# Thirteen places of twelve matmuls for the local branch's output products, and a shorter sum in the final norm

## The chip, the cores and the metric

The kernel runs on one core of a Trainium2 chip. A core has a matrix engine (TensorE, in the profile PE, its weight loads PEld), an engine for elementwise work and reductions (VectorE, DVE), one for activation functions and copies (ScalarE, ACT), a general one (GpSimd, POOL), and one that issues transfers (SyncE, SP). They run side by side and wait for one another by semaphores. Matmuls write to PSUM, which is handed out here in banks of 128 x 512 float32; everything else lives in SBUF.

The metric is the device time of the whole program in microseconds, the median of several runs. Before the change it is 1325.01 us (three runs: 1324.27, 1325.01 and 1326.56).

## The reference

One decoder layer on a sequence of 1024 positions with 1024 channels, all in float32, with two attention branches that are mixed by gates. Cut to what matters:

```
h = rmsnorm(x, mix_norm_g)
qa, ka, va, q_lat, kv_lat, k_r, g_a, g_b = split(h @ w_in)
o_a = sliding-window attention of qa, ka, va          # "local", 8 heads of 64
o_b = causal latent attention, 8 heads, softmax over all earlier positions
y   = sigmoid(g_a) * (o_a @ w_o_swa) + sigmoid(g_b) * (o_b @ w_o_mla)
x   = x + y @ w_out
h   = rmsnorm(x, ffn_norm_g)
x   = x + (silu(h @ w_gate) * (h @ w_up)) @ w_down
out = x * rsqrt(mean(x * x) + 1e-6) * final_norm_g
```

The change touches the product `o_a @ w_o_swa` with its gate `sigmoid(g_a)`, in its place in the program alone, and the last line.

## The kernel before

**Products in three passes.** Every float32 operand is split into a high part and a rest (`split`: ScalarE copies, line 163, VectorE subtracts, line 166), and `mm3` (lines 172 to 174) makes three matmuls of each pair: high by high, high by rest, rest by high. A product of 128 x 512 over 512 input channels is therefore twelve matmuls of 512 columns.

**The latent steps.** After the projections and the local attention the kernel goes through the latent attention in 64 steps `t`: 8 heads `h` by 8 query blocks of 128, where `n = t % 8` counts the steps of a head. The blocks of a head are taken in the order 2, 3, 6, 7, 0, 1, 4, 5, so a step handles between 128 and 1024 key positions. In program order a step does this:

- `scores(t + 2)`: the scores of the step after next on TensorE (lines 1253 to 1255) into one of two double banks of PSUM (`scb`); VectorE adds the mask and takes the row maximum in one instruction (line 1263), ScalarE takes the exponential and its sum (1264), GpSimd the reciprocal of the sum as a power (1265) and scales the probabilities `p` with it (1266).
- `pv` for a pair of blocks whose `p` was transposed some steps earlier (lines 1302, 1303, the result in `ob`).
- in certain steps, part of a unit of the local branch's output product (`mix_a`, matmuls into `oA`).
- `transposes(t)`: the blocks of `p` of this step by TensorE (line 1280, into `pTb`), then the split by ScalarE and VectorE (`pth`, `ptl`).
- loads and conversions for later steps.

So the softmax of a step runs on VectorE, ScalarE and GpSimd while TensorE does the work of two steps, and the transposition is where TensorE comes back to its result.

**The local branch's output products.** There are 16 units `(dc, sh)`: 8 blocks of 128 output channels by 2 halves of the positions, twelve matmuls each. When a unit is complete, VectorE multiplies it by the gate in one instruction (line 1359; the gate tile `sg` holds tanh(g / 2), to which 1 is added, twice the sigmoid). Thirteen units lie among the latent steps, three behind them or in the last step. In the kernel before each of the thirteen is cut in two halves of six matmuls (`c0 = 0` and `c0 = 2`), and the 26 halves have places in the dictionary `fill`: steps 5 and 6 of head 0; n = 1, 2, 5 and 6 of heads 1, 3 and 5; n = 1, 2 and 5 of heads 2, 4, 6 and 7. Between its halves a unit keeps its bank, one of the four of the pool `P1`, which also serves `pTb` and `ob`.

For every other unit a new gate tile is loaded (`load_sig`, line 1333, 512 KB, dictionary `g_at`, at the place ahead of the unit's first) and ScalarE turns it into the tanh (`twice_sigmoid`, line 1336) in the unit's first step, behind the transpositions. The weights come in four pieces, loaded six steps and converted two steps ahead of the unit that first uses them (`w_at`).

**Order.** In this stretch the order of the instructions on each engine isn't written out by hand. A planner makes it at compile time from the program order and its own estimate of the durations, and an instruction that it takes to be ready can be put ahead of an earlier one. Instructions traced under `held[0] = True` keep their program order. On the chip each engine then runs its list strictly in that order.

**The end.** The last stage is the product with `w_down`, in seven products of half size (`ORDER` is 1, 6, 2, 7, 5, 4, 3). When the products 4 and 3 are through, each of four tiles of 128 rows goes through the final norm (`down_done`, `final`): VectorE adds the residual (line 180), ScalarE squares one half of the channels and sums (1931), GpSimd divides by 1024 and adds the other half's sum, which already holds the epsilon (1936), GpSimd takes the power -1/2 (1937), then VectorE and ScalarE multiply one half each (1939, 1942), and both are stored. The other half's sum was prepared by `first_half` at products 2 and 5.

Of the kernel before, what the change touches and what calls it, by code (L numbers as in the profile page):

```python
# [8 lines left out]
F32 = mybir.dt.float32  # L9
# [8 lines left out]
P = 128  # L18
S = 1024
D = 1024  # L20
# [69 lines left out]
def hybrid_block_kernel(  # L90
# [53 lines left out]
    def U(name, dt=F32, shape=(P, 1024)):  # L144
        return pool.tile(list(shape), dt, tag="u", name=uid(name))
# [7 lines left out]
    def P1(name, shape=(P, 512), dt=F32):  # L153
        return ps1.tile(list(shape), dt, tag="ps", name=uid(name))
# [212 lines left out]
    def bcast_gain(name, g, w=1024):  # L367
        t = U(name)
        nc.sync.dma_start(t[:, 0:w], g.partition_broadcast(P))
        return t  # L370
# [964 lines left out]
    def twice_sigmoid(g):  # L1335
        a = nc.scalar.activation(g, g, AF.Tanh, scale=0.5)
        if held[0]:
            tc.keep_in_program_order(a)
# [4 lines left out]
    def mix_a(dc, sh, c0, n, ps=None):  # L1343
        if ps is not None:
            oa_ps[(dc, sh)] = ps
        ps = oa_ps[(dc, sh)]
        if (sh, c0) == (0, 0):
            if dc >= 4:
                ar[dc] = gate[dc]
            elif dc % 2 == 0:  # L1350
                t = V("ar", F32, (P, 2, S))
                ar[dc], ar[dc + 1] = t[:, 0], t[:, 1]
            if dc % 2 == 0:
                wo[dc // 2] = st.get(("oa", dc // 2))
        w = wo[dc // 2]
        mm3(ps, [((w[0][:, c, blk(dc % 2)], w[1][:, c, blk(dc % 2)]), oaT[(c, sh)]) for c in range(c0, c0 + n)],
            c0 == 0, c0 + n == 4)
        if c0 + n == 4:
            nc.vector.scalar_tensor_tensor(ar[dc][:, half(sh)], gate[dc][:, half(sh)], 1.0, oa_ps.pop((dc, sh)),
                                           op0=ALU.add, op1=ALU.mult)  # L1360
            if sh == 1:
                gate.pop(dc)
                if dc >= 4:
                    nc.sync.dma_start(ar_d[dc - 4], ar.pop(dc))
# [55 lines left out]
    load_k(2)  # L1420
    first = {0: (2, 0), 1: (2, 1), 2: (3, 0), 3: (3, 1)}
    fill = {}
    units = [(u // 2 ^ 4, u % 2, c) for u in range(16 - 3) for c in (0, 2)]
    slots = [5, 6] + [NB * h + n for h in range(1, NH) for n in (1, 2, 5, 6) if n < 6 or h in (1, 3, 5)]
    for t, u in zip(slots, units):
        fill[t] = u
    w_at = {t: u[0] // 2 for t, u in fill.items() if u[0] % 2 == 0 and u[1:] == (0, 0)}
    g_at = {a: fill[b][0] for a, b in zip([3] + slots, slots) if fill[b][1:] == (0, 0)}
    g_at[NT - 3] = 3
    pvq = []  # L1430
    OUT_AT = {34: 0, 40: 1, 43: 2, 47: 3, 50: 4, 54: 5, 58: 6}
    for t in range(NT):
        h, n = divmod(t, NB)
        if t + 2 < NT:
            scores(t + 2)
        while pvq and pvq[0][0] <= t:
            pv(*pvq.pop(0)[1:])
        if n == 4 and h + 2 < NH:
            load_q(h + 2)
        if n == 6 and h + 3 < NH:  # L1440
            load_k(h + 3)
        hh, nn = step(t)
        if nn % 2 == 1:
            pvq.append((t + 3, hh, nn // 2))
        e = t - (NT - 8)
        if e == 6:
            psum_phase("psc", 4)
        if t in first:
            prod_k(*first[t])
        if t in fill:  # L1450
            dc, sh, c0 = fill[t]
            mix_a(dc, sh, c0, 2, P1("oA") if c0 == 0 else None)
        if t == NT - 1:
            mix_a(13 // 2 ^ 4, 13 % 2, 0, 4, PX("oA"))
        transposes(t)
        if t in OUT_AT:
            out_sums(OUT_AT[t])
        held[0] = True
        if t in g_at:
            load_sig(g_at[t])  # L1460
        if t in fill and fill[t][1:] == (0, 0):
            twice_sigmoid(gate[fill[t][0]])
        if t == NT - 1:
            twice_sigmoid(gate[3])
        if t == 3:
            load_oa(0, 1)
            load_oa(1, 1)
        if t < 4 or 6 <= t < 10:
            split_oa(t % 4 // 2 if t < 4 else (t - 6) // 2, t // 6, t % 2)
        if t + 6 in w_at or t == 0:  # L1470
            st.load_to(st.index[("oa", w_at.get(t + 6, 2))])
        if t + 2 in w_at:
            st.conv_to(st.index[("oa", w_at[t + 2])])
        if e == 4:
            load_sigs(DCS[0])
        if -3 <= e < 3:
            split_ob((e + 3) // 2, (e + 3) % 2)
        if e in (2, 6):
            st.load_to(st.index[("ob", 0 if e == 2 else 2)])
        if e == 6:  # L1480
            st.conv_to(st.index[("ob", 0)])
        held[0] = False
# [441 lines left out]

    p1, u2, u3 = V("dp1"), V("du2"), V("du3")
    fing = bcast_gain("fing", fin_g)
    fin_s = const.tile([P, 2, 2, 4], F32, name="fin_s")

    def sumsq(i, d, t):
        junk = U("sq", F32, (P, 512))  # L1930
        nc.scalar.activation(junk, xq[(i, d)][:, t], AF.Square, accum_out=fin_s[:, i, d, t:t + 1])

    def final(i, t, d):

        fs = fin_s[:, i, d, t:t + 1]
        nc.gpsimd.tensor_scalar(fs, fs, 1.0 / D, fin_s[:, i, 1 - d, t:t + 1], op0=ALU.mult, op1=ALU.add)
        nc.gpsimd.tensor_tensor(fs, fs, neg_half, op=ALU.pow)
        y = xq[(i, d)][:, t]
        nc.vector.scalar_tensor_tensor(y, y, fs, fing[:, half(d)], op0=ALU.mult, op1=ALU.mult)
        nc.sync.dma_start(out[blk(4 * i + t), half(d)], y)  # L1940
        y = xq[(i, 1 - d)][:, t]
        nc.scalar.mul(y, y, fs)
        nc.scalar.dma_start(out[blk(4 * i + t), half(1 - d)], y)

    def first_half(i, t, d):

        fs = fin_s[:, i, d, t:t + 1]
        nc.gpsimd.tensor_scalar(fs, fs, 1.0 / D, EPS, op0=ALU.mult, op1=ALU.add)
        y = xq[(i, d)][:, t]
        nc.gpsimd.tensor_tensor(y, y, fing[:, half(d)], op=ALU.mult)  # L1950

# [2 lines left out]
    def down_done(q, t):  # L1954
        ps = banks["A" if q in (1, 2, 5, 3) else "B"][t]
        if q == 1:
            nc.scalar.copy(p1[:, t], ps)
        elif q == 6:
            add(u2[:, t], ps, p1[:, t], nc.vector)
            add(u2[:, t], u2[:, t], xq[(0, 1)][:, t], nc.gpsimd)  # L1960
        elif q == 7:
            add(u3[:, t], ps, p1[:, t], nc.vector)
            add(u3[:, t], u3[:, t], xq[(1, 1)][:, t], nc.gpsimd)
            add(p1[:, t], p1[:, t], xq[(1, 0)][:, t], nc.gpsimd)
        else:
            i, d = {2: (0, 0), 5: (1, 1), 4: (1, 0), 3: (0, 1)}[q]
            x_ = xq[(i, d)][:, t]
            add(x_, ps, {2: x_, 5: u3[:, t], 4: p1[:, t], 3: u2[:, t]}[q], nc.vector)
            sumsq(i, d, t)
            if q in (4, 3):  # L1970
                final(i, t, d)
            else:
                first_half(i, t, d)
# [127 lines left out]
```

## Time and profile before

| | us |
|---|---|
| median of the runs | 1325.01 |
| the profiled execution's own time | 1323.36 |
| its span, first to last instruction | 1320.8 |
| granted TensorE clock | 0.998 of full speed |
| ScalarE busy in the span | 635.7 |
| GpSimd busy in the span | 560.8 |

The latent steps run from about 383 us to 550 us of the span. The profile gives for each engine when it was busy, for each group of instructions the mean duration and what ended the idle time ahead of it, and a chain of waits followed back from the last instruction. A row of the view in order of time reads: start in us, length in us, engine, line, operation, output <- inputs, shape, count, and in brackets the idle time ahead of it with what ended that. The matmuls are pipelined and their ends are modelled, so the distance from start to start tells more than the length.

### The profile page before, as it was taken

What the parts mean: (1) busy time and instruction counts of PE and PEld (TensorE: products, weight loads), DVE (VectorE), ACT (ScalarE), POOL (GpSimd) and SP (SyncE); (2) the same over time, 40 slices, a digit from 0 to 9 for tenths busy, and PEclk for the clock granted to TensorE, in tenths of its full rate; (3) what the DMA queues carried; (4) which work ended last, traced back from release to release, by engine and by line L of the source; (5) the groups of instructions that cost most, each with busy time, mean ns of one, the idle gap of its engine ahead of it and who ended that gap; (6) DMA issues with size and microseconds to landing.
All of it is one profiled execution on the core that took longest, in us unless ns stands there. A gap on an engine that the chain in (4) does not pass through costs nothing.

```text
span 1320.8 us, 19066 instructions
## 1 busy us (share of the span) xinstructions
PE 1308.5 (99%) x6516; PEld 1102.8 (83%) x6516; DVE 916.1 (69%) x1509; ACT 635.7 (48%) x1289; POOL 560.8 (42%) x623
## 2 busy tenths in 40 slices
PE   9999999999999999999999999999999999999997
PEld 6899888888888888888888888888888888888886
DVE  7868687786767777877779655756666554663962
ACT  7434667675456666654455232332223323644452
POOL 2115546552325556312232465777567631022521
PEclk9999999999999999999999999999999999999999
DMA  9454444456576478898521334655554435996503
GB/s 375 161 187 160 133 161 138 154 177 215 164 250 181 104 216 192 266 306 199 185 112 48 124 135 162 233 201 197 184 183 148 147 120 197 373 375 226 175 20 140
DMA packets 92192, 245.12 MB, mean 186 GB/s; under 512 B 10304, under 2 KB 17984, under 8 KB 90944
## 3 DMA queue, kind: packets, MB, share of 16 engines
q1 hardware_dynamic: 87264, 233.15, 51.0%
q0 software_dynamic: 3392, 8.39, 3.6%
q10 hardware_dynamic: 1440, 2.36, 0.5%
q8 instruction: 52, 0.85, 0.3%
q14 instruction: 44, 0.36, 0.1%
HBM read 161.16 MB, written 78.51 MB: 181 GB/s over the span
## 4 chain that ended last, share of the span: by engine, by line
PE 60%; POOL 2%; issue 2%; DVE 2%; ACT 1%; DMA 0%; POOLq 0%; DVEq 0%; SPq 0%; ACTq 0%
PE fa L172 6%; PE fa L174 6%; PE fa L173 6%; PE fd L173 5%; PE fd L174 5%; PE fd L172 5%; PE fb L173 5%; PE fb L174 5%; PE fb L172 5%; PE xo L174 2%; PE xo L173 2%; PE xo L172 2%; POOL p L1266 1%; POOL denb L1265 1%; PE oB L174 1%
## 5 line engine op out<-in xcount | busy, mean ns | idle before, releaser
L166 DVE TENSOR_TENSOR wl<-wr,wl 128x512 fp32r<-128x512 f32 x150 | 144.3, 986 | 74.0 <-ACT wl L163 73.5
L166 DVE TENSOR_TENSOR lrv<-lr,lrv 128x1024 fp32r<-128x1024 f32 x77 | 105.2, 1397 | 49.4 <-ACT lrv L163 43.4
L163 ACT CAST lrv<-lr 128x1024 fp32r<-128x1024 f32 x77 | 80.1, 1052 | 94.1 <-PE fd L174 52.2
L172 PE MATMUL fd<-lrv 128*128 128x512 f32 x308 | 119.8, 389 | 0.0
L173 PE MATMUL fd<-lrv 128*128 128x512 f32 x308 | 119.8, 389 | 0.0
L174 PE MATMUL fd<-lrv 128*128 128x512 f32 x308 | 119.8, 389 | 0.0
L177 POOL TENSOR_TENSOR wr<-wr,sm 128x512 f32<-128x512 f32 (+1 forms) x38 | 45.6, 1209 | 137.9 <-DVE wl L166 119.6
L163 ACT CAST wl<-wr 128x512 fp32r<-128x512 f32 x150 | 86.5, 621 | 3.8 <-DVE t3l L177 2.8
L166 DVE TENSOR_TENSOR wl<-sm,wl 128x512 fp32r<-128x512 f32 x60 | 50.3, 862 | 42.8 <-ACT wl L163 42.6
L1265 POOL TENSOR_TENSOR denb<-denb,neg_one 128x1 f32<-128x1 f32 x64 | 39.9, 623 | 92.6 <-ACT p L1264 80.7
L172 PEld LDWEIGHTS fd<-lrv 128*128 128x128 f32 x308 | 57.8, 188 | 12.1
L173 PEld LDWEIGHTS fd<-lrv 128*128 128x128 f32 x308 | 57.8, 188 | 12.0
L174 PEld LDWEIGHTS fd<-lrv 128*128 128x128 f32 x308 | 57.8, 188 | 11.9
L1264 ACT ACTIVATE p<-scb,nmb 128x384 f32<-128x384 f32 (+3 forms) x64 | 47.7, 746 | 32.0 <-DVE nmb L1263 24.9
L361 POOL TENSOR_SCALAR ms<-ss 128x1 f32<-128x1 f32 x32 | 8.6, 269 | 122.8 <-ACT xn L1742 45.5
L1263 DVE CUSTOM_DVE_ANT_0 scb<-scb,mask 128x384 f32<-128x384 f32 (+3 forms) x64 | 48.4, 761 | 17.4 <-PE scb L1255 16.4
L1638 ACT ACTIVATE act<-sm 128x512 f32<-128x512 f32 x11 | 7.0, 633 | 102.2 <-DVE sm L180 102.2
L166 DVE TENSOR_TENSOR ptl<-pTb,pth 128x512 fp32r<-128x512 f32 (+2 forms) x96 | 50.0, 550 | 8.0 <-ACT pth L163 7.8
L163 ACT CAST pth<-pTb 128x512 fp32r<-128x512 f32 (+2 forms) x96 | 43.4, 480 | 18.2 <-PE pTb L1280 17.2
L1266 POOL TENSOR_SCALAR p<-p,denb 128x384 f32<-128x384 f32 (+3 forms) x64 | 48.4, 756 | 6.3
L1638 ACT ACTIVATE act<-pu 128x512 f32<-128x512 f32 x22 | 13.9, 632 | 69.7 <-DVE pu L180 69.7
L172 PE MATMUL fa<-t1h,wl 128*128 128x512 f32 x120 | 47.1, 392 | 0.1
(354 smaller groups left out, 4291.0 us busy)
## 6 DMA issues: line engine op xcount, KB each, us to landing
lr<-la_d SPq DMA_DIRECT2D x77, 256.0 KB, 5.3
wr<-in_w_gate_dram SPq DMA_DIRECT2D x22, 512.0 KB, 4.4
wr<-in_w_up_dram SPq DMA_DIRECT2D x22, 512.0 KB, 5.1
la_d<-sd SPq DMA_DIRECT2D x22, 512.0 KB, 4.9
wd<-in_w_down_dram SPq DMA_DIRECT2D x22, 512.0 KB, 7.0
rb_d<-wd SPq DMA_DIRECT2D x22, 512.0 KB, 2.7
lr<-rb_d SPq DMA_DIRECT2D x44, 256.0 KB, 5.4
lr<-in_w_down_dram SPq DMA_DIRECT2D x33, 256.0 KB, 5.3
```

Source lines behind the costliest of these rows:

```text
L163: i = nc.scalar.copy(hi, src)
L166: (eng or nc.vector).tensor_tensor(lo, src, hi.bitcast(F32), op=ALU.subtract)
L172: nc.tensor.matmul(ps, ah, bh, start=first and i == 0, stop=False, skip_group_check=go_on)
L173: nc.tensor.matmul(ps, ah, bl, start=False, stop=False, skip_group_check=go_on)
L174: nc.tensor.matmul(ps, al, bh, start=False, stop=last and i == n - 1, skip_group_check=go_on)
L177: eng.tensor_tensor(out, a, b, op=ALU.subtract)
L361: nc.gpsimd.tensor_scalar(ms, ss, 1.0 / width, EPS, op0=ALU.mult, op1=ALU.add)
L1263: nc.vector.tensor_tensor_reduce(s_, s_, m_, 1.0, -NEG, op0=ALU.add, op1=ALU.min, accum_out=nm)
L1264: nc.scalar.activation(p_, s_, AF.Exp, scale=-1.0, bias=nm, accum_out=den)
L1265: nc.gpsimd.tensor_tensor(den, den, neg_one[:, 0:1], op=ALU.pow)
L1266: nc.gpsimd.tensor_scalar(p[:, 0:w], p[:, 0:w], den, 0.0, op0=ALU.mult, op1=ALU.add)
L1638: nc.scalar.activation(dst, src, AF.Silu)
```

## The change

The thirteen units are no longer cut. Each stands as twelve matmuls in one place: step 6 of head 0 and then n = 2 and n = 6 of heads 1 to 6 (step 54 is the last). The gate's load stands three steps ahead of its unit's first place in all cases, and the tanh one step ahead, behind that step's transpositions. The pieces of weights keep their distances of six and two steps, so they move with the units.

In the final norm the gain is multiplied once by the square root of 1024, so that the sums of squares need no division: `first_half` makes sum + 1024 * epsilon. In the last product (number 3) VectorE instead of ScalarE forms the sum of squares, with one instruction that starts from the other half's sum, and the result goes straight into the power. In product 4 GpSimd adds the two halves.

```diff
-    units = [(u // 2 ^ 4, u % 2, c) for u in range(16 - 3) for c in (0, 2)]
-    slots = [5, 6] + [NB * h + n for h in range(1, NH) for n in (1, 2, 5, 6) if n < 6 or h in (1, 3, 5)]
+    units = [(u // 2 ^ 4, u % 2, 0) for u in range(16 - 3)]
+    slots = [6] + [NB * h + n for h in range(1, 7) for n in (2, 6)]
...
-    g_at = {a: fill[b][0] for a, b in zip([3] + slots, slots) if fill[b][1:] == (0, 0)}
+    g_at = {b - 3: fill[b][0] for b in slots if fill[b][1:] == (0, 0)}
...
-            mix_a(dc, sh, c0, 2, P1("oA") if c0 == 0 else None)
+            mix_a(dc, sh, c0, 4, P1("oA"))
...
-        if t in fill and fill[t][1:] == (0, 0):
-            twice_sigmoid(gate[fill[t][0]])
+        if t + 1 in fill and fill[t + 1][1:] == (0, 0):
+            twice_sigmoid(gate[fill[t + 1][0]])
...
     fing = bcast_gain("fing", fin_g)
+    nc.scalar.mul(fing, fing, D ** 0.5)
...
+    def sumsq_v(i, d, t):
+        junk = U("sq", F32, (P, 512))
+        y = xq[(i, d)][:, t]
+        nc.vector.tensor_tensor_reduce(junk, y, y, 1.0, fin_s[:, i, 1 - d, t:t + 1], op0=ALU.mult, op1=ALU.add,
+                                       accum_out=fin_s[:, i, d, t:t + 1])
+
     def final(i, t, d):
 
         fs = fin_s[:, i, d, t:t + 1]
-        nc.gpsimd.tensor_scalar(fs, fs, 1.0 / D, fin_s[:, i, 1 - d, t:t + 1], op0=ALU.mult, op1=ALU.add)
+        if (i, d) == (1, 0):
+            nc.gpsimd.tensor_tensor(fs, fs, fin_s[:, i, 1 - d, t:t + 1], op=ALU.add)
         nc.gpsimd.tensor_tensor(fs, fs, neg_half, op=ALU.pow)
...
-        nc.gpsimd.tensor_scalar(fs, fs, 1.0 / D, EPS, op0=ALU.mult, op1=ALU.add)
+        nc.gpsimd.tensor_scalar(fs, fs, 1.0, D * EPS, op0=ALU.mult, op1=ALU.add)
...
-            sumsq(i, d, t)
+            if q == ORDER[-1]:
+                sumsq_v(i, d, t)
+            else:
+                sumsq(i, d, t)
```

## The prediction

> **What bounds the kernel now.** I read the page's busy times first, then a table of windows that cuts the latent steps at the first transposition of each head, then the order of TensorE's and GpSimd's instructions in time, and last the chain of waits at the end of the span.
>
> ```profile
> PE 1308.5 (99%) x6516; PEld 1102.8 (83%) x6516; DVE 916.1 (69%) x1509; ACT 635.7 (48%) x1289; POOL 560.8 (42%) x623
> ```
>
> TensorE is the bound over the span. What the change moves lies in the latent steps, so their limit has to be read there. The next view has a row for each of heads 1 to 7: window and length, then busy time and instructions of PE, PEld, DVE, ACT and POOL, granted clock, DMA share, GB/s.
>
> ```profile
> 404.95:427.28 22.33, 21.61 (x138) 18.80 (x138) 18.04 (x37) 15.05 (x36) 11.58 (x16) 1.00 0.59 146
> 427.28:447.89 20.61, 19.96 (x133) 17.65 (x132) 15.43 (x34) 14.64 (x34) 11.06 (x16) 1.00 0.59 145
> 447.89:468.93 21.04, 21.00 (x139) 18.63 (x137) 14.62 (x34) 12.80 (x30) 10.33 (x16) 1.00 0.44 135
> 468.93:489.31 20.38, 19.91 (x132) 17.53 (x132) 13.82 (x31) 13.20 (x32) 10.31 (x16) 1.00 0.72 213
> 489.31:510.15 20.84, 20.84 (x139) 18.71 (x138) 15.88 (x35) 14.74 (x34) 12.42 (x18) 1.00 0.79 176
> 510.15:530.44 20.29, 20.24 (x134) 17.77 (x134) 15.61 (x34) 15.09 (x35) 11.68 (x17) 1.00 0.66 159
> 530.44:550.28 19.84, 19.10 (x124) 16.65 (x124) 17.81 (x34) 14.76 (x32) 11.62 (x15) 1.00 0.76 204
> ```
>
> Odd heads 1, 3 and 5 have four places of six output products, heads 2, 4 and 6 three. The heads with 24 products (3 and 5; head 1 also waits for weights) took 21.04 and 20.84 us, mean 20.94. Those with 18 took 20.61, 20.38 and 20.29, mean 20.43. Six products more cost 0.51 us, though a product takes 0.23 us of TensorE:
>
> ```profile
> 463.80 0.45 PE L172 MATMUL oA<-wv,wv 128*128 128x512 f32 x1
> 464.08 0.39 PE L173 MATMUL oA<-wv,wv 128*128 128x512 f32 x1
> 464.31 0.39 PE L174 MATMUL oA<-wv,wv 128*128 128x512 f32 x1
> ```
>
> From start to start a product takes 464.31 - 464.08 = 0.23 us, six 1.4 us. So a head with 18 holds 1.4 - 0.51 = 0.9 us in which TensorE waits without much of it showing as idle: products there are partly cover for the softmax. The idle time in the rows, length less PE busy, is 0.65, 0.47 and 0.05 us in heads 2, 4 and 6.
>
> Here a rule is to be weighed. The Trainium skill, "Trainium Kernel Development and Optimization", section Performance Expectations, calls matmul busy time a bad metric because matmuls are pipelined. The rows agree: the idle column has 0.4 us a head on average, the lengths tell of 0.9. By the idle column the 18 products that move into heads 2, 4 and 6 would cost 3 x 1.4 - 1.17 = 3.0 us instead of 1.5, and the sum below would end at +0.5.
>
> **The change part by part.** All 156 products of these thirteen units stay, so TensorE's work is the same. Five things differ there, and one at the end.
>
> *Heads.* After the change head 1 to 6 have 24 products each, head 7 none of these (its last unit of twelve, at step 63, stays). Heads 2, 4 and 6 get six more: 3 x 0.51 = +1.5 us; at worst, unhidden, 3 x 1.4 = +4.2. Head 7 loses 18: at most -4.2 us, and by the same rate as above (0.51 for six) only -1.5; it could be nothing if its softmax chain sets the pace. Head 7 is the head in which VectorE is fullest, 17.81 of 19.84 us (90%). It sheds two evictions there (line 1359, at steps 57 and 61), and one conversion of weights, which comes at step 52 instead of 56; that favours the upper half. I take -2.5. Sum -1.0, ends -2.7 and +4.2.
>
> *Steps 1 and 5 of a head.* They lose their six products, so the transpositions come 1.4 us earlier behind the same softmax. GpSimd's scaling of p ends the softmax of a step; here those of steps 33, 37 and 41 (head 4, n = 1 and 5; head 5, n = 1), and then the transpositions that wait for them:
>
> ```profile
> 470.64 0.70 POOL L1266 TENSOR_SCALAR p<-p,denb 128x512 f32<-128x512 f32 x1
> ...
> 480.67 0.48 POOL L1266 TENSOR_SCALAR p<-p,denb 128x256 f32<-128x256 f32 x1
> ...
> 490.47 0.69 POOL L1266 TENSOR_SCALAR p<-p,denb 128x512 f32<-128x512 f32 x1
> ```
>
> ```profile
> 472.62 0.60 PE L1280 MATMUL pTb<-ident_r,p 128*128 128x128 f32 x4
> ...
> 482.74 0.39 PE L1280 MATMUL pTb<-ident_r,p 128*128 128x128 f32 x2
> ...
> 491.73 0.60 PE L1280 MATMUL pTb<-ident_r,p 128*128 128x128 f32 x4
> ```
>
> p was ready at 471.34, 481.15 and 491.16, so the slack is 1.28, 1.59 and 0.57 us. Less 1.4 that is a wait of 0.12, none, and 0.83. A wait here delays everything behind it on TensorE: the next scores, hence VectorE's maxima and the exponentials. Six heads at 0.83 give the upper end, +5.0. The lower end is 0, for the planner may draw products of step n = 2 or 6 in front of such a transposition. It has done so: the place of the next products was step 57, and two ran ahead of the transpositions of step 56:
>
> ```profile
> 530.21 0.40 PE L173 MATMUL oA<-wv,wv 128*128 128x512 f32 x1
> 530.44 0.52 PE L1280 MATMUL pTb<-ident_r,p 128*128 128x128 f32 x3
> ```
>
> Two of the three slacks lose next to nothing, so I take +1.4, 0.12 in each of twelve steps.
>
> *Groups.* There are thirteen groups fewer to enter. The first product above is 464.08 - 463.80 = 0.28 us ahead of its successor, 0.05 over the later ones: 13 x 0.05 = -0.65, ends 0 and -0.65.
>
> *The PSUM bank.* Six units had their halves three or four steps apart (21 and 25, 26 and 29, 30 and 33, 34 and 37, 53 and 57, 58 and 61) and kept one of four banks all that while; the transposed blocks want banks of the same four. The waits view of the stage (us in total, times, longest) has, for a transposition behind an eviction:
>
> ```profile
> PEld pTb L1280 <- DVE ptl L166: 0.8, 3, 0.3
> ```
>
> Some of that goes: -0.5, ends 0 and -0.8.
>
> *The gate's load and sigmoid.* The load is always three steps ahead of its unit now and the sigmoid one step ahead, so two steps, 2 x 20.4 / 8 = 5.1 us, lie between. From issue to landing it takes (KB each, median us):
>
> ```profile
> sg<-gate_d SPq DMA_DIRECT2D x12, 512.0 KB, 5.3
> ```
>
> ScalarE would wait a few tenths, with the exponentials of the next steps queued behind the sigmoid, and the scores for their PSUM. Before, the load for the unit that begins at step 30 stood only one step ahead, and TensorE idled behind it once:
>
> ```profile
> 469.96 0.50 PE L1253 MATMUL scb<-kT,qT 96*128 96x512 f32 x1 [0.29 <-ACT p L1264]
> ```
>
> So -0.3 if none is late, 6 x 0.29 - 0.3 = +1.4 if all six later ones are; I take 0. On SyncE's queue the load now always stands just ahead of the next head's queries (n = 4), which are wanted twelve steps later and can stand the half microsecond of its issue.
>
> *The end.* After the last matmul one tile goes through the final norm:
>
> ```profile
> 1314.48 0.73 ACT sq L1931 x2
> 1315.21 0.09 issue
> 1315.31 0.27 POOL fin_s L1936
> 1315.57 0.04 issue
> 1315.61 0.60 POOLq L2097
> 1316.22 0.02 issue
> 1316.24 0.75 DVE xq L1939
> ```
>
> The 0.60 holds the power. ScalarE's square (0.73) becomes VectorE's sum of products, and the 0.27 + 0.04 of line 1936 go. The same instruction on 512 columns stands in the latent steps (with the reading of its accumulator):
>
> ```profile
> L1263 DVE DVE_READ_ACCUMULATOR2_ANT nmb<- 128x1 f32 x54 | 7.5, 140 | 0.0
> ...
> L1263 DVE CUSTOM_DVE_ANT_0 scb<-scb,mask 128x512 f32<-128x512 f32 x6 | 4.1, 691 | 2.1 <-PE scb L1255 2.1
> ```
>
> 0.69 + 0.14 = 0.83, 0.10 more than ScalarE's. So 0.10 - 0.31 = -0.2 us. There one operand was in PSUM; two from SBUF are bounded above by the page's
>
> ```profile
> L166 DVE TENSOR_TENSOR wl<-wr,wl 128x512 fp32r<-128x512 f32 x150 | 144.3, 986 | 74.0 <-ACT wl L163 73.5
> ```
>
> 0.99 + 0.14 - 0.73 - 0.31 = +0.1; below, no reason excludes 0.1 less than the row, so -0.3. The Trainium skill, "GPSIMD Engine Reference", section Specifications, says that VectorE instructions with two SBUF inputs contend with GpSimd for its interface; by that the 986 would belong to stretches with GpSimd at work. At the end GpSimd is waiting for this very sum, so by the rule -0.2 stands, and without it +0.1 could. The other tiles of the last product lie behind matmuls. The new scaling of the gain is one ScalarE pass over 1024 columns (the conversion of line 163 took 1.05 for that size on the page) after its load at 1102.6 and before
>
> ```profile
> L1950 POOL TENSOR_TENSOR xq<-xq,fing x8: 1294/1303/2172, 1193.9 to 1259.7; 128x512 f32<-128x512 f32 x8
> ```
>
> its first use at 1193.9: hidden by 90 us of matmuls; uncovered it would cost 1 us. GpSimd's addition for the product before the last replaces an instruction on one column by one, behind matmuls too.
>
> **Sum.** -1.0 + 1.4 - 0.65 - 0.5 + 0 - 0.2 = -0.95 us. The span goes from 1320.8 to 1319.8; its execution took 1323.36, and the median of the runs is 1325.01, so 1324.0 in terms of the median.
>
> **The rivals.** *Slower: head 7 doesn't give back what heads 2, 4 and 6 take.* Without products head 7 is paced by its softmax chain and stays near 19.8 us, while the others pay 1.4 each: +4.2 + 1.4 - 0.65 - 0.5 - 0.2 = +4.25, 1329.3. For it: VectorE's 90% and 0.74 us of idle TensorE there. Against: VectorE sheds work in just that head, and the rate of 0.51. It decides once head 7 shortens by less than some 1.6 us with the 4.2 paid in full.
>
> *Faster: head 7 gives back all 4.2*, the steps n = 1 and 5 are filled by products drawn forward, and the bank's waits go: +1.5 - 4.2 - 0.65 - 0.8 - 0.2 = -4.35, 1320.7. For it: the two products of step 57 drawn forward, VectorE's relief. Against: 0.57 us of slack at step 41.
>
> *The places are only nominal.* The planner orders TensorE's work by its own estimate, and the order comes out much as before; then the end alone is left: -0.2, 1324.8. For it: products already ran outside their places. Against: in head 7 there is nothing left to draw.
>
> **How the numbers follow.** About 0.2% (2.65 us) is what a measurement of this kernel can tell from no change: 1322.36 to 1327.66. Forecast 0.40, with its own range 1321.5 to 1326.5; slower rival 0.21; faster rival 0.29; nominal 0.10. Of the forecast 0.06 falls below 1322.36 and 0.02 above 1327.66. Faster 0.29 + 0.06 = 0.35, slower 0.21 + 0.02 = 0.23, the same 0.42. Range 1319.0 to 1329.0: it takes in most of both rivals.
>
> **What would show it.** In the windows by head: heads 2, 4 and 6 near 20.9 us, head 7 near 17.3. Transpositions at n = 1 and 5 should start within 0.2 us of the end of GpSimd's scaling, or have products drawn ahead of them. At the end no line 1936 in the chain, and about 1.6 us instead of 1.78 between VectorE's addition (which ended 0.02 us before the square) and its last product. It is wrong if head 7 stays over 19 us, if a sigmoid holds ScalarE by more than half a microsecond in several heads, or if a later stage, whose instructions the change leaves alone, changes its length by over 1 us.

## The result and the profile after

The changed kernel takes 1342.81 us (median of four runs, 1341.88 to 1343.96), beside 1325.58 us for the kernel before on the same chip: a ratio of 1.0139, 95% interval 1.0127 to 1.0150, so about 18 us or 1.4% slower. The profiled execution took 1342.25 us, its span is 1339.8 us against 1320.8. The prediction of 1324.0 us, range 1319.0 to 1329.0, did not hold.

The busy times on the page of after hardly tell of it:

```profile
PE 1314.4 (98%) x6516; PEld 1107.5 (83%) x6516; DVE 919.1 (69%) x1517; ACT 635.0 (47%) x1282; POOL 555.4 (41%) x619
```

TensorE has the same 6516 matmuls and is 5.9 us busier, and the span is 19.0 us longer. The table of windows by head says where. Columns as before; each row runs from the first transposition of a head to that of the next, the last one to the first transposition of step 63. Heads 4 to 7 of after, then head 7 of before in that same measure:

```profile
471.39:498.34 26.95, 22.55 (x139) 19.73 (x138) 15.99 (x35) 14.71 (x34) 11.66 (x18) 0.95 0.59 166
498.34:528.34 30.00, 24.22 (x137) 21.16 (x138) 14.40 (x33) 13.70 (x31) 12.87 (x19) 0.84 0.58 141
528.34:550.06 21.72, 21.64 (x137) 19.28 (x138) 15.74 (x34) 15.31 (x34) 10.64 (x16) 0.97 0.47 121
550.06:568.66 18.60, 15.75 (x105) 13.33 (x105) 15.54 (x30) 13.32 (x30) 11.13 (x15) 1.00 0.73 188
```

```profile
530.44:549.74 19.30, 18.56 (x120) 16.11 (x119) 17.27 (x33) 14.76 (x32) 11.62 (x15) 1.00 0.75 198
```

Head 4 went from 20.38 to 26.95 us and head 5 from 20.84 to 30.00: 15.7 us in two heads, and their granted clock is 0.95 and 0.84 where it was 1.00. All eight heads together take 18.0 us more. Heads 4 and 5 are where to look, and ScalarE's instructions in order of time show one thing there that before had nowhere (in brackets the idle time of the engine and what ended it):

```profile
492.08 1.06 ACT L1336 ACTIVATE sg<-sg 128x1024 f32<-128x1024 f32 x1 [4.96 <-DMA sg<-gate_d]
...
520.07 1.06 ACT L1336 ACTIVATE sg<-sg 128x1024 f32<-128x1024 f32 x1 [8.61 <-DMA sg<-gate_d]
521.03 0.88 ACT L1264 ACTIVATE p<-scb,nmb 128x768 f32<-128x768 f32 x1
```

Two tanh instructions wait 4.96 and 8.61 us for the transfer of their gate, and ScalarE, which keeps its order, does nothing else meanwhile. The exponential behind the second starts as soon as the tanh is over. In before the tanh that belong to these gates ran without any idle time ahead of them:

```profile
492.85 1.06 ACT L1336 ACTIVATE sg<-sg 128x1024 f32<-128x1024 f32 x1
...
515.15 1.07 ACT L1336 ACTIVATE sg<-sg 128x1024 f32<-128x1024 f32 x1
```

The transfers are late for two reasons, which SyncE's queue shows (after):

```profile
479.79 1.23 SPq L338 DMA_DIRECT2D wt_d<-in_w_out_dram  x2
481.14 0.52 SPq L1333 DMA_DIRECT2D sg<-gate_d  x1
...
509.96 0.50 SPq L338 DMA_DIRECT2D wt_d<-wt_d  x1
510.57 0.52 SPq L1333 DMA_DIRECT2D sg<-gate_d  x1
```

and the same queue before:

```profile
462.59 0.38 SPq L1333 DMA_DIRECT2D sg<-gate_d  x1
463.02 1.33 SPq L338 DMA_DIRECT2D wt_d<-in_w_out_dram  x2
...
500.34 0.34 SPq L1333 DMA_DIRECT2D sg<-gate_d  x1
501.83 0.50 SPq L338 DMA_DIRECT2D wt_d<-wt_d  x1
```

Line 338 belongs to another job that runs through these steps: sums of blocks of `w_out` are prepared in DRAM, by copies on SyncE and adding transfers on GpSimd (line 329), at the steps of the dictionary `OUT_AT`, which the change left alone. In before a gate's load stands ahead of the copies. In after the first load comes right behind two copies of 1 MB and lands 10.9 us after its issue (issued at 481.14, the tanh starts at 492.08). In before, with the same copies right behind it instead of ahead, the load of 462.59 took 5.6 us. The second stands behind a copy that must itself wait for GpSimd's adding transfer. The chain of waits of after has both, one behind the other (its longest pieces alone):

```profile
501.89 8.06 DMA wt_d<-in_w_out_dram
510.57 9.48 DMA sg<-gate_d
520.12 0.92 issue
521.03 1.54 ACT p L1264 x4
524.04 1.51 PE pTb L1280 x6
```

The Trainium skill, "DMA: Bandwidth & Descriptors", section "Queues, rings and completion order", says that each DMA engine takes the descriptors of a ring in their order; the 10.9 us behind the copies and the 5.6 us ahead of them agree with that.

What waits behind the tanh on TensorE (after, in order of time):

```profile
494.61 0.97 PE L1280 MATMUL pTb<-ident_r,p 128*128 128x128 f32 x6 [4.29 <-DVE ob L1314]
...
522.06 0.80 PE L1253 MATMUL scb<-kT,qT 96*128 96x512 f32 x1 [5.34 <-ACT p L1264]
```

At 494.61 the wait is for a PSUM bank that VectorE frees after a copy of ScalarE, at 522.06 for the exponential itself. These 9.6 us are not all. The windows of 3 us in and behind the second stall (same columns as above, the granted clock is the third number from the end):

```profile
517.00:520.00 3.00, 0.00 (x0) 0.00 (x0) 0.00 (x0) 0.00 (x0) 0.00 (x0) 0.90 1.00 228
520.00:523.00 3.00, 0.94 (x2) 0.84 (x3) 0.00 (x0) 2.90 (x6) 0.81 (x2) 0.50 0.92 232
523.00:526.00 3.00, 2.67 (x10) 1.89 (x9) 2.76 (x7) 1.76 (x5) 1.74 (x3) 0.50 0.06 14
526.00:529.00 3.00, 3.00 (x13) 2.81 (x12) 2.11 (x6) 0.81 (x3) 1.24 (x2) 0.50 0.00 0
529.00:532.00 3.00, 3.00 (x19) 2.63 (x19) 1.00 (x1) 2.05 (x4) 1.57 (x2) 0.90 0.00 0
```

TensorE stood still for 5.34 us, and for about 9 us the clock granted to it is half. The Trainium skill, "TensorE: Matmul & The Clock Gate", section "HAM oscillation — how this bites in real kernels", sets the bound at idle gaps of some 3.4 us; the gaps of 4.29 and 5.34 us here lie above it, and the clock fell with both (after the first, a window shows 0.52). But it also fell after gaps of 1.70 and 2.10 us, in the control kernel further down, so in this case a shorter gap is enough, and the measurement decides. An estimate from the windows above: from 522.06 to about 529.6 us TensorE works at half the clock, worth some 3.8 us; with the 5.34 us that is 9.1 us, beside the 9.16 us by which head 5 grew.

At the end of the kernel, the last tile's chain from the sum of squares on (after, in order of time):

```profile
1333.84 0.75 DVE L1937 CUSTOM_DVE_ANT_0 sq<-xq,fin_s 128x512 f32<-128x512 f32 x1
1334.51 0.08 DVE L1937 DVE_READ_ACCUMULATOR2_ANT fin_s<- 128x1 f32 x1
1334.68 0.55 POOL L1945 TENSOR_TENSOR fin_s<-fin_s,neg_half 128x1 f32<-128x1 f32 x1 [2.85 <-DVE fin_s L1937]
...
1335.26 0.75 DVE L1947 SCALAR_TENSOR_TENSOR xq<-xq,fin_s,fing 128x512 f32<-128x512 f32 x1 [0.66 <-POOL fin_s L1945]
```

From the start of the sum to the end of the last product 2.17 us (1333.84 to 1336.01), where before has 2.51 (from 1314.48 to 1316.24 + 0.75). This part did what it says.

### The profile page after: what moved, and what is told of

Same layout as the page of the kernel before. It is cut to its first block, busy times and chain, and to the rows that moved or that the text cites. A ratio compares the mean times of both kernels' runs of the same rounds, so it can differ in the third digit from the quotient of the medians.

```text
span 1339.8 us, 19041 instructions
## 1 busy us (share of the span) xinstructions
PE 1314.4 (98%) x6516; PEld 1107.5 (83%) x6516; DVE 919.1 (69%) x1517; ACT 635.0 (47%) x1282; POOL 555.4 (41%) x619
## 4 chain that ended last, share of the span: by engine, by line
PE 88%; issue 3%; POOL 3%; DVE 2%; DMA 2%; ACT 1%; SPq 0%; POOLq 0%; DVEq 0%; ACTq 0%
PE fa L172 8%; PE fa L174 8%; PE fa L173 8%; PE fb L173 6%; PE fb L172 6%; PE fb L174 6%; PE fd L172 5%; PE fd L173 5%; PE fd L174 5%; PE xo L172 2%; PE xo L174 2%; PE xo L173 2%; POOL p L1266 1%; POOL denb L1265 1%; PE oB L173 1%
## 5 line engine op out<-in xcount | busy, mean ns | idle before, releaser
L1280 PE MATMUL pTb<-ident_r,p 128*128 128x128 f32 x288 | 44.4, 280 | 7.1 <-DVE ob L1314 4.6
```

The lines of the kernel that those rows point to most:

```text
L1280: nc.tensor.transpose(pp[:, i], p[:, blk(k0 + i)], ident)
```

## The experiments

The theory after this reading: the two late gates cost most of the 18 us, through ScalarE's order. Rivals: the tanh's new place in the step costs, whatever the load does; the twelve products in a row cost; the loss comes with the norm's new passes. All ratios are to the kernel before, run in the same job, with their 95% intervals. Results first:

| kernel | median us | ratio |
|---|---|---|
| norm alone | 1323.53 | 0.9998 (0.9989 to 1.0007) |
| first load two steps earlier | 1337.22 | 1.0093 (1.0080 to 1.0107) |
| second load two steps earlier | 1334.07 | 1.0068 (1.0054 to 1.0081) |
| both loads two steps earlier | 1327.81 | 1.0024 (1.0015 to 1.0033) |
| the `w_out` sums moved instead | 1327.78 | 1.0021 (1.0012 to 1.0030) |
| kernel before with late loads | 1329.42 | 1.0031 (1.0017 to 1.0045) |
| whole units, head 7 used too | 1328.04 | 1.0027 (1.0017 to 1.0037) |
| whole units at n = 1 and 5 | 1326.87 | 1.0019 (1.0009 to 1.0030) |
| halves in the even spread | 1323.94 | 1.0000 (0.9991 to 1.0008) |
| quarters | 1326.16 | 1.0014 (1.0005 to 1.0022) |
| tanh behind the product | 1332.49 | 1.0058 (1.0044 to 1.0073) |
| tanh in the unit's own step | 1337.40 | 1.0087 (1.0064 to 1.0110) |
| halves, one more unit in head 7 | 1322.33 | 0.9981 (0.9970 to 0.9993) |
| halves, two more units in head 7 | 1321.74 | 0.9977 (0.9964 to 0.9989) |

**The norm alone**: the latent steps of before, with the new final norm.

> The latent steps of the kernel before, with the new final norm alone. Theory (late gates: two tanh instructions hold ScalarE for gate loads that stand behind the w_out transfers): the norm is worth -0.3 us, 1325.3. Rival (the norm takes part in the loss): over 1328. The chain at the end has no addition by GpSimd ahead of the power.

Ratio 0.9998: the 0.34 us of the last tile are below what the runs tell, and the norm has no part in the loss.

**One load at a time, then both.** The changed kernel, with one line edited; the three new lines are the three kernels (the units at steps 38 and 46 use the late gates):

```diff
-    g_at = {b - 3: fill[b][0] for b in slots if fill[b][1:] == (0, 0)}
+    g_at = {33 if b == 38 else b - 3: fill[b][0] for b in slots if fill[b][1:] == (0, 0)}
+    g_at = {41 if b == 46 else b - 3: fill[b][0] for b in slots if fill[b][1:] == (0, 0)}
+    g_at = {b - 5 if b in (38, 46) else b - 3: fill[b][0] for b in slots if fill[b][1:] == (0, 0)}
```

> The changed kernel with the gate load for step 38 at step 33, ahead of the two w_out copies, and nothing else moved. Theory late gates: the wait of 5.0 us goes and head 4 shrinks from 26.95 to about 21.5 us, the wait of 8.6 us stays: 1342.8 - 5.4 = 1337.4. Rival (the places of twelve themselves: products missing at n = 1 and 5 and in head 7): within 2 us of 1342.8.

> The changed kernel with the gate load for step 46 at step 41, which puts it ahead of the copy that waits for GpSimd's sum. Theory late gates: the wait of 8.6 us goes, head 5 shrinks from 30.0 to about 21.5, the wait of 5.0 stays: 1342.8 - 8.5 = 1334.3. Rival (the places): within 2 us of 1342.8.

> The changed kernel with both gate loads moved (steps 33 and 41). Theory late gates: the two gains add, 1342.8 - 13.9 = 1328.9, granted clock back at 1.00 in heads 4 and 5. Rival (the places): still over 1340.

With the first load earlier head 4 takes 21.52 us and head 5 still 29.91; with the second alone head 4 takes 26.53 and head 5 21.06. With both no tanh waits, the clock is 1.00 in every head, and 1327.81 us remain. 1342.81 - 1327.81 = 15.0 us are the late gates (by the ratios 1.0139 - 1.0024, 15.2): by heads 13.8 (184.76 us for the eight in after, 170.95 with both loads earlier). In all three the tanh stays where the change put it, so its place alone is not what costs, or the loss would have stayed.

**The other side of the same queue.** The loads stay at the steps that after gives them; the jobs of line 338 move out of their way:

```diff
-    OUT_AT = {34: 0, 40: 1, 43: 2, 47: 3, 50: 4, 54: 5, 58: 6}
+    OUT_AT = {38: 0, 41: 1, 45: 2, 51: 3, 53: 4, 56: 5, 59: 6}
```

> The changed kernel with its gate loads where it has them, but the w_out copies and sums some steps later (38, 41, 45, 51, 53, 56, 59), so that they stand behind both gate loads on SyncE's queue. Theory late gates: as with both loads moved, about 1328 us, and no tanh that waits over 1 us. Rival (the loads are late for another reason, their own distance of three steps): still over 1335.

1327.78 us: the same gain without touching a gate. The median time from issue to landing of the gates' loads between 455 and 535 us (KB each, median us), in after and here:

```profile
sg<-gate_d SPq DMA_DIRECT2D x4, 512.0 KB, 6.8
```

```profile
sg<-gate_d SPq DMA_DIRECT2D x4, 512.0 KB, 4.1
```

So it isn't the distance of two steps that is too short, but that distance behind those transfers.

**The same fault put into the kernel before**: its halves and its tanh, with two loads (those of `0` and `1`) where they meet the copies:

```diff
-    g_at = {a: fill[b][0] for a, b in zip([3] + slots, slots) if fill[b][1:] == (0, 0)}
+    g_at = {3: 4, 10: 0 + 5, 18: 6, 29: 7, 38: 0, 46: 1, 57: 2}
...
-    OUT_AT = {34: 0, 40: 1, 43: 2, 47: 3, 50: 4, 54: 5, 58: 6}
+    OUT_AT = {37: 0, 40: 1, 43: 2, 45: 3, 50: 4, 54: 5, 58: 6}
```

> The kernel before, halves in their 26 places, with two gate loads put behind w_out transfers on SyncE's queue: the load for the unit of step 41 at step 38 behind the two copies (now at step 37), the load for that of step 49 at step 46 behind the copy that waits for GpSimd's sum (now at step 45). Theory late gates: the same stall comes without any change of the places, two tanh instructions wait for their loads and heads 5 and 6 grow, 5 to 14 us over the kernel before. Rival (the places): within 2 us of the kernel before.

Measured 1329.42, by the ratio some 4 us. ScalarE's tanh in that run:

```profile
470.58 1.06 ACT L1336 ACTIVATE sg<-sg 128x1024 f32<-128x1024 f32 x1 [1.52 <-DMA sg<-gate_d]
500.41 1.07 ACT L1336 ACTIVATE sg<-sg 128x1024 f32<-128x1024 f32 x1 [1.85 <-DMA sg<-gate_d]
```

Waits of 1.52 and 1.85 us lengthen heads 4 and 5 to 22.94 and 24.85 us at a clock of 0.93. Only the second wait belongs to a load that I made late: issued at 489.68 right behind the two copies, it took 10.7 us. The first belongs to the load of step 29, which stands only one step ahead of its tanh here as in before and has no copy ahead of it; it took 7.0 us instead of 5.6, and the cause of that stays open. The other load that I made late (9.8 us to landing) still came in time. So a tanh that waits for its gate costs time in this kernel too, and one of its two waits comes from the copies. The size was below the expected one, for the tanh stands one step later behind its load than in after.

**The tanh a step later.** Two kernels leave the late loads and delay the tanh. In the first it stands in the unit's step behind the product:

```diff
-        if t + 1 in fill and fill[t + 1][1:] == (0, 0):
-            twice_sigmoid(gate[fill[t + 1][0]])
+        if t in fill and fill[t][1:] == (0, 0):
+            twice_sigmoid(gate[fill[t][0]])
```

> The changed kernel with one thing undone: the tanh stands again in the unit's own step, one step (2.6 us) later on ScalarE than in the changed kernel; the loads stay where the change put them. Theory (the tanh is late because the load is, and ScalarE keeps its order): the waits of 4.96 and 8.61 us shrink by about 2.6 to some 2.4 and 6.0 us, and heads 4 and 5 lose less: 24 to 25.5 and 27 to 28.5 us instead of 26.95 and 30.00; time 1337 to 1340. Rival (the sigmoid's place in the step, ahead of other work of ScalarE, is what costs, not the load): the loss goes away in full, 1328; or it stays in full, 1342.8, if the load's time decides nothing.

I had overlooked that a whole unit ends in the step in which it begins: VectorE's product (line 1359) now read the gate ahead of the tanh, so this kernel multiplies the first half of the positions of each block by 1 plus the raw gate (and in blocks 4 to 7, whose product is written over the gate, takes the tanh of that product), and the tanh waits for VectorE instead of the load. Its 1332.49 us decide nothing about the question. The second puts the tanh ahead of the product in that step:

```diff
         if t in fill:
             dc, sh, c0 = fill[t]
+            if (sh, c0) == (0, 0):
+                held[0] = True
+                twice_sigmoid(gate[dc])
+                held[0] = False
```

> The changed kernel with the tanh in the unit's own step, ahead of the unit's product that reads it, one step (2.6 us) later on ScalarE than the change has it; the loads stay where the change put them. Theory (the tanh waits because the load lands late, and ScalarE keeps its order): the waits of 4.96 and 8.61 us shrink by some 2.6 to about 2.4 and 6.0, heads 4 and 5 to 24 to 26 and 26 to 29 us; time 1336 to 1340. Rival (the sigmoid's place on ScalarE is what costs): the loss is gone, 1328, or untouched, 1342.8.

```profile
ACT sg L1336 <- DMA sg<-gate_d: 9.0, 2, 5.1
```

The waits view (us in total, times, longest) has 9.0 us where after has 13.6; heads 4 and 5 take 26.21 and 26.85 us, and the time is 1337.40. The second wait shrank by 3.5 us (8.61 to 5.07), the first by 1.0 (4.96 to 3.96) where 2.6 were expected, and head 4 came out just above its range. A later tanh waits less and costs less, as it must if the landing is what it waits for.

**What is left without late gates: 1.0024.** Three theories. A: head 7 without products wastes waits that other heads then pay for. B: steps n = 1 and 5 miss their products. C: twelve products in one place fill the waits of neighbouring steps worse than six. For A the whole units go to n = 2 of heads 1 to 7 and n = 6 of heads 1 to 5, for B to n = 1 and 5, both with loads five steps ahead (the two new lines, A first):

```diff
-    slots = [6] + [NB * h + n for h in range(1, 7) for n in (2, 6)]
+    slots = [6] + [NB * h + n for h in range(1, 8) for n in (2, 6) if n == 2 or h < 6]
+    slots = [6, 10, 13] + [NB * h + n for h in range(2, 7) for n in (1, 5)]
```

> Thirteen whole units, all gate loads five steps ahead, with the units of step 54 and of step 50 moved: places n = 2 of heads 1 to 7 and n = 6 of heads 1 to 5, so head 7 has one unit and head 6 one. On top of late gates 3.7 us are left between the kernel with both loads moved (1327.8) and the kernel before. Theory A (head 7 without products is where they go: it gave back 0.7 us of 4.2): 2 to 3 us of them come back, 1325.3. Theory B (n = 1 and 5 without products, in all heads): within 1 us of 1327.8.

> Thirteen whole units, all gate loads five steps ahead, at n = 1 and 5 of heads 2 to 6 (and steps 6, 10 and 13) instead of n = 2 and 6, head 7 empty as in the changed kernel. Theory B (the transpositions at n = 1 and 5 wait for a softmax that nothing covers, 0.3 to 0.6 us a step): 3 us come back, 1324.8. Theory A (head 7): within 1 us of 1327.8.

A is out: head 6 gives 2.6 us and head 7 takes 2.2 (20.82), ratio 1.0027. B isn't it either: with the products at n = 1 and 5 the heads still take 21.2 to 21.7 us, for now n = 2 and 6 have none. Nor do the earlier loads matter by themselves: heads 2 to 5 take 85.99 us in A's kernel, with all loads five steps ahead, and 85.89 with two of them moved. For C the even spread of the change stays, in halves (n = 1, 2, 5, 6 of heads 1 to 6), then in quarters (one in each of steps 6 to 57):

```diff
-    units = [(u // 2 ^ 4, u % 2, 0) for u in range(16 - 3)]
-    slots = [6] + [NB * h + n for h in range(1, 7) for n in (2, 6)]
+    units = [(u // 2 ^ 4, u % 2, c) for u in range(16 - 3) for c in (0, 2)]
+    slots = [5, 6] + [NB * h + n for h in range(1, 7) for n in (1, 2, 5, 6)]
...
-    g_at = {b - 3: fill[b][0] for b in slots if fill[b][1:] == (0, 0)}
+    g_at = {max(b - 5, 1): fill[b][0] for b in slots if fill[b][1:] == (0, 0)}
...
-            mix_a(dc, sh, c0, 4, P1("oA"))
+            mix_a(dc, sh, c0, 2, P1("oA") if c0 == 0 else None)
```

> The changed kernel's even spread (24 products in each of heads 1 to 6, none in head 7), but in 26 places of six as before, at n = 1, 2, 5 and 6, with gate loads five steps ahead so that no tanh waits. Theory C (twelve products in a row fill the waits of a step worse than six): heads 3 and 5, which then do what they did before, go back to 21.0 and 20.8, heads 2, 4 and 6 stand near 21.0 instead of 21.5 to 21.9, head 7 stays near 18.6; sum about 168.0 against 170.95 with both gates repaired, so 3 us under it: about 1325.0. Rival (the even spread itself costs it: a head of 24 products takes 21.4 or more, whatever their grouping): heads 2, 4 and 6 stay at 21.4 to 21.9, time 1327 to 1328.

> The same products in 52 places of three, one in each step from 6 to 57, gate loads five steps ahead. Theory C carried on: still finer places fill the waits no worse than places of six, so 1324 to 1325.5, heads 1 to 6 at 20.6 to 21.2. Rival: each place has a price of its own (a start of a group and a change of operands, and the eviction's bank is held over four steps instead of one), so that the sum is above that of the places of six: over 1327.

Halves give 1.0000, with the new norm in it. Heads 3, 6 and 7 with whole units and both loads repaired, then with halves:

```profile
450.92:472.33 21.41, 21.12 (x139) 18.83 (x138) 14.40 (x33) 13.71 (x33) 10.37 (x16) 1.00 0.53 145
...
515.20:537.12 21.92, 21.54 (x138) 18.70 (x138) 16.75 (x36) 15.82 (x36) 11.85 (x17) 1.00 0.59 151
537.12:555.71 18.59, 15.72 (x104) 13.32 (x104) 15.55 (x30) 13.32 (x30) 11.16 (x15) 1.00 0.73 197
```

```profile
449.27:469.89 20.62, 20.62 (x138) 18.69 (x138) 14.48 (x33) 13.58 (x33) 10.29 (x16) 1.00 0.36 109
...
511.66:532.76 21.10, 20.87 (x138) 18.76 (x138) 16.95 (x35) 15.14 (x36) 12.29 (x17) 1.00 0.72 171
532.76:551.38 18.62, 15.73 (x104) 13.32 (x104) 15.48 (x30) 13.30 (x30) 11.16 (x15) 1.00 0.72 194
```

Same matmuls in each pair, 0.8 us apart in heads 3 and 6, while head 7, without units in both, is the same. C holds against whole units in the change's places, and the step n = 1 of head 3 shows how. Whole units, then halves, in order of time (PEld is the load of a matmul's weights):

```profile
452.67 0.60 PE L1280 MATMUL pTb<-ident_r,p 128*128 128x128 f32 x4
...
453.35 0.19 PEld L1253 LDWEIGHTS scb<-kT,qT 96*128 96x128 f32 x1 [0.32 <-ACT p L1264]
```

```profile
452.16 0.39 PE L174 MATMUL oA<-wv,wv 128*128 128x512 f32 x1
...
452.40 0.60 PE L1280 MATMUL pTb<-ident_r,p 128*128 128x128 f32 x4
...
452.75 0.30 PE L1253 MATMUL scb<-kT,qT 96*128 96x128 f32 x1
```

What is late in a step without products is not the transposition but the next scores: they need a double bank that the exponential of an earlier step must have read. With six products ahead of the transposition the scores follow it by 0.35 us, without them by 0.68. The waits views of heads 2 to 6, whole units, then halves:

```profile
PEld scb L1253 <- ACT p L1264: 3.7, 11, 0.4
```

```profile
PEld scb L1253 <- ACT p L1264: 1.3, 3, 0.4
```

That is 2.4 us less, and the five heads differ by 3.2 (107.81 against 104.60). The weight loads overlap the matmuls, so the two figures need not add up one to one; that this wait is most of the difference is argued, not shown. With whole units at n = 1 and 5 it is small too (2.8 us over all heads, where n = 2 and 6 have 5.5 and the halves 2.3); there the transpositions wait for the bank of `ob` (2.7 us, 0.2 in the other two). So twelve in one place cost in both kernels, by different waits as far as these views show.

Quarters (1.0014) are between. In heads 2 to 6 they take 104.71 us, as much as halves; the rest lies in head 0 (23.00 us against 21.45) and head 7 (19.14 against 18.62), which got other steps. So the runs show that twelve in a place are worse than six, not that three are.

**Head 7.** If its softmax binds it, products put there should cost little, and units that stand from the last step on, where matmuls follow each other every 0.23 us, could move in. From the kernel of halves, one unit more (two more take all of `[57, 58, 61, 62]`, unit 15 the last step, and leave `rest` empty):

```diff
-    units = [(u // 2 ^ 4, u % 2, c) for u in range(16 - 3) for c in (0, 2)]
-    slots = [5, 6] + [NB * h + n for h in range(1, 7) for n in (1, 2, 5, 6)]
+    units = [(u // 2 ^ 4, u % 2, c) for u in range(16 - 2) for c in (0, 2)]
+    slots = [5, 6] + [NB * h + n for h in range(1, 7) for n in (1, 2, 5, 6)] + [57, 58]
...
-    g_at[NT - 3] = 3
+    g_at[NT - 6] = 3
...
-            mix_a(13 // 2 ^ 4, 13 % 2, 0, 4, PX("oA"))
+            mix_a(14 // 2 ^ 4, 14 % 2, 0, 4, PX("oA"))
...
-        if t == NT - 1:
+        if t == NT - 2:
             twice_sigmoid(gate[3])
...
-    rest = [(i // 2 ^ 4, i % 2) for i in range(14, 16)]
+    rest = [(i // 2 ^ 4, i % 2) for i in range(15, 16)]
```

> The kernel of halves in an even spread, with one more unit in the steps: unit 13 in two halves at n = 1 and 2 of head 7 (12 products), unit 14 in the last step, unit 15 behind it, the place of the last unit in the stage behind the steps empty; the third load of a gate goes three steps earlier. Theory (head 7 gave back only 0.7 of 4.2 us because its softmax chain binds it, so its products cost little either way): head 7 rises by 0.3 to 0.7 over 18.62, while the stage behind the steps, where products follow each other every 0.23 us, loses 12 x 0.23 = 2.7: 2.0 to 2.4 under the kernel of halves, about 1321.7, ratio 0.998 to the kernel before. Rival (products in head 7 cost what products cost in heads 1 to 6, or what the step's arithmetic says, 0.23 each): head 7 at 20.5 or more, time 1323.5 to 1324.5.

> Two more units in the steps: units 13 and 14 in four halves at n = 1, 2, 5 and 6 of head 7, unit 15 in the last step, nothing of them behind it. Theory: 24 products in head 7 cost 1.0 to 2.2 (heads 3 and 5 with as many stand 2.0 over the empty head 7), and 24 x 0.23 = 5.5 go from behind the steps, less what the second unit there covered (the wait for the last output products of the heads, up to 2.7): 0.6 to 4 under the kernel of halves, 1320 to 1323. Rival (the unit behind the last step was cover for its softmax chain): PE idles there by 2 to 3 us and the time is 1324 or more.

Head 7 with one unit and with two:

```profile
532.64:551.88 19.24, 18.18 (x116) 15.66 (x116) 16.18 (x31) 14.48 (x31) 11.00 (x15) 1.00 0.72 201
```

```profile
531.52:552.98 21.46, 20.69 (x129) 17.80 (x128) 17.79 (x33) 14.39 (x31) 11.05 (x15) 1.00 0.73 216
```

Twelve products cost 0.62 us in head 7 (19.24 - 18.62), 24 cost 2.84; a unit behind the steps takes 12 x 0.23 = 2.8. Both kernels come out some 0.2% below the kernel before, at 0.9981 and 0.9977 with intervals that end under 1; the two can't be told apart. The second unit costs 2.2 us and saves 2.8, so it gains little; the 2.84 us for both are more than the 1.0 to 2.2 expected.

## Why the prediction was wrong

**The gate's load and sigmoid: this step failed.** It was costed at 0 with ends -0.3 and +1.4, and it costs 15.0 us by the medians. The prediction set 5.1 us of distance against a median landing of 5.3 and concluded "ScalarE would wait a few tenths". That is wrong in two parts. A median over twelve loads says nothing of a load at a place where none stood before: it left out line 338 on SyncE's queue, and the two loads that matter took 10.9 and 9.48 us. For the first the dictionaries told of it beforehand: the copies stand at step 34, the load at step 35. And the dictionary's three steps are program order, not the queue's: the planner put a copy of step 47, which waits for GpSimd, ahead of the second load of step 43. It was free to, because line 1333 doesn't ask for program order, though it is traced under `held[0] = True`; the tanh does (lines 1337 and 1338). The prediction looked at what the load is moved in front of (the next head's queries) and not at what it is moved behind. What it left out besides is the price of a stall: it was taken as its own length, while TensorE's 9.6 us of idle came with half the clock behind them.

**Heads: wrong sign.** Predicted -1.0: +1.5 for heads 2, 4 and 6, -2.5 for head 7. By the kernel of halves, which isolates the spread, heads 2, 4 and 6 take 0.50, 0.73 and 0.81 us more, so +2.0, near the rate of 0.51 taken; head 7 gives 0.68 (19.30 to 18.62). The rate measured on heads that carry 18 or 24 products doesn't hold for a head brought to none: TensorE is then busy for 15.7 of 18.6 us, and twelve products put back cost only 0.62 us, so the softmax chain seems to set the pace, as the slower rival said. VectorE's relief in that head (17.27 to 15.48 us busy), which spoke for the upper half, did not bring it. Yet the even spread in halves loses nothing in sum: heads 0, 1, 3 and 5 are 0.2 to 0.5 us shorter each there, which no run explains.

**Steps 1 and 5, groups and bank.** Predicted +1.4 - 0.65 - 0.5 = +0.25 for all three; whole units against halves cost +3.2 in heads 2 to 6. The uncovered steps were seen, with an end of +5.0 that holds this; the wait was misnamed. The slack was taken between GpSimd's scaling and the transposition, where the waits are small (0.7 us in these heads with whole units); the larger wait (3.7 us) is for the exponential, ahead of the scores. Nothing in the runs shows the gain from fewer groups or from the bank by itself.

**The end: right, a little more than said.** -0.34 instead of -0.2 us: the sum takes 0.75 us and its reading lies inside that, not behind it. The bound of +0.1 from line 166's 0.99 us did not occur.

**The rivals.** The slower one described what is left without late gates quite well: it gave 4.25 us over the kernel before, and the kernel with both loads repaired has a ratio of 1.0024, so 3.2 us (by heads 4.23, 170.95 less 166.72). Its parts fit less well than its sum, which is in part luck: heads 2, 4 and 6 take 3.75 us of the 4.2, head 7 gives 0.7 where the rival had nothing, and head 0, which it left out, takes 0.8. And it left the gates out as the forecast did, so neither reached 1342.8. The faster one is out, as head 7 gave 0.7 of 4.2 us, and the places are not nominal: head 7 holds 105 matmuls where before has 120. The condition "head 7 stays over 19 us" did not occur (18.60), the one on a sigmoid holding ScalarE did, in two heads.

The sum as measured, by heads: 13.8 late gates, 4.2 twelve instead of six (head 0 among them), 0.1 the even spread, together the 18.0 us.

## What to carry to other kernels

Before a load is moved, list what stands ahead of it on its queue at the new place, in the queue's own order, with what those transfers wait for; a median landing time holds only for the places it was measured at. An instruction on an engine that keeps its order, moved ahead of other work, turns each microsecond of a late load into one for all behind it, and a stall of TensorE of some microseconds is paid again in clock. In this softmax pipeline fill work in pieces of six matmuls, in twice as many steps, cost less than in pieces of twelve, and a head that got no filler at all gave back little of what left it.

## What was not expected of the hardware

The stall's second price: after 5.34 us without a matmul, the clock was 0.50 for about 9 us, and matmuls on 512 columns started 0.43 us apart (after, in order of time) where 0.23 is usual:

```profile
525.78 0.63 PE L1254 MATMUL scb<-kT,qT 96*128 96x512 f32 x1
526.21 0.63 PE L1255 MATMUL scb<-kT,qT 96*128 96x512 f32 x1
```

In the control kernel, whose tanh waited for only 1.52 and 1.85 us, TensorE stood still for less (in order of time):

```profile
472.36 0.50 PE L1253 MATMUL scb<-kT,qT 96*128 96x512 f32 x1 [1.70 <-ACT p L1264]
...
503.28 1.71 PE L1280 MATMUL pTb<-ident_r,p 128*128 128x128 f32 x8 [2.10 <-DVE ob L1314]
```

Still the granted clock was 0.50 from 473 to 476 us and from 504 to 506.5. Its mean is 0.93 in both heads, and these are 2.6 and 4.0 us longer than in before, for 3.4 us of ScalarE's waits together.
